# A list scheduler's choice on TensorE: 16-bit products ahead of float32 ones

## The chip, the cores and the metric

The kernel runs on one core of a Trainium2 chip. The metric is device time in microseconds (us); lower is better. Times are medians over runs, and one execution was also taken by the hardware profiler.

## The reference, cut to what matters

One step of an encoder trunk with one layer (`DEPTH = 1`) over 2048 prompt frames and 64 frames of a running stream, width 1024:

```python
h = rmsnorm(x, norm1_w)
proj = h @ w_in
# ... q, k, v (causal convolution, SiLU), z, decay a, beta b, pooling input u_pool
o, s_new = gated_delta_chunked(q, k, v, g, beta, s_prev, chunk)      # 4 heads of 128
o_delta = rmsnorm(o, onorm_w) * silu(z)
o_pool, pool_new = multiscale_pool(u_pool, pool_prev, pos0, pool_w, pool_scale)
x = x + concatenate([o_delta, o_pool]) @ w_out
h = rmsnorm(x, norm2_w)
x = x + (silu(h @ w_gate) * (h @ w_up)) @ w_down                     # d_ff = 2816
return rmsnorm(x, normf_w), ...                                      # and the new states
```

In `gated_delta_chunked` each chunk of a head needs the inverse `T` of a unit lower triangular matrix `eye + Lm`, and the state `S` is carried from chunk to chunk in order:

```python
T = triangular_solve(eye + Lm, eye)
...
v_new = u_c - w_c @ S
o_c = qd_c @ S + qk_c @ v_new
S = S * dl_c + kt_c.T @ v_new
```

## The kernel before, in words

The kernel first notes its instructions and only then issues them. Every call such as `nc.tensor.matmul(...)` goes to `Machine.note`, which records the operation with its predecessors, a cost and a rank. At the end `Machine.issue` walks through a planned time: at each step it takes the engine that can go first, takes one of that engine's ready operations, and sets down when it starts. The order in which operations are taken is the order in which each engine runs them on the chip. All of them are issued from one line, L278, so the profile's rows are told apart by their tiles.

The rank is the number under which an operation was noted, less a boost. Fronts and heads (below) are noted with a boost of 100000, so they have negative ranks and go ahead of the projections. A tile of a pool is given to an operation only when the planned time has freed one of that tag's buffers.

TensorE runs three kinds of products, set in `Machine.cost`: `"r"`, float32r operands; `"h"`, 16-bit operands; `"f"`, float32 operands and transposes. `Machine.pick` chooses among TensorE's ready ones. Products that are not `"r"` go ahead, but only in groups: while the last product was `"r"` and another `"r"` is ready, they are held until `HOLD` us after one of them became ready (0.4 for boosted ones, 3.0 for others). Once one has gone, the others that are ready follow it, by rank, until none is left.

The work has two parts.

- *First part, to about 945 us.* Four blocks of tokens (576, then three of 512). For each block: the input projection (`pp`, float32r, each operand split into a high and a low part, three products for one), four heads, four pooling groups, and the out-projection (`pz`) of the block before it, between the block's own projections. The last two blocks' out-projections come at the end; the third block's operands go through DRAM (`od`) and are loaded and split again (`op<-od`).
- *Second part.* Gate, up and down products in float32r (`px`, `py`, `pz`, `d`, `dx`, `dy`, `dz`), in a form with seven products in place of eight.

A head has two `Front`s, each for two chunks of 128 frames, and one serial chain. A front makes transposes (`ptk`, `ptv`, float32), Gram products (`gr`, float32), row sums (`gb`), and then doubles the inverse in seven levels (`py`, `pt`), with a correction (`pf`, `px` with the suffix `_p`); these levels are 16-bit. Between two of its products stands an operation of DVE or ACT that takes the result out of PSUM. The serial chain (`Head.prompt`) makes, for each chunk, the products `pk` (three) and `po` (two) in float32 with an ACT or DVE step between them, and ends with sums over squares (`os`, float32r) and a norm. A front's results wait in buffers (`NOUT = 5` and `NX = 3` of them) until the serial chain has used them.

Of the kernel before, what the change touches and what calls it, by code (L numbers as in the profile page):

```python
# [58 lines left out]
class Machine:  # L59
# [6 lines left out]
    def __init__(self, nc):  # L66
        self.nc, self.ops, self.seen, self.boost, self.n = nc, [], {}, 0, 0
        self.tiles, self.slots, self.queue, self.parked, self.later, self.early = {}, {}, {}, {}, {}, 0
        self.free = {e: 0.0 for e in ("tensor", "vector", "scalar", "gpsimd", "sync")}
        self.last, self.at = None, 0.0  # L70
        self.busy = {"vector": 0.0, "gpsimd": 0.0}
        self.wire = 0.0
        self.gone = 0.0
        for e in self.free:
            setattr(self, e, Engine(self, e))
# [205 lines left out]
    def pick(self, ready, t):  # L281

        others = sorted(x for x in ready if x[2].kind != "r")
        if others:
            first = others[0]
            held = self.last == "r" and len(others) < len(ready) and t < min(x[2].ready + HOLD[x[0] >= 0] for x in others)
            if held:
                first = min(x for x in ready if x[2].kind == "r")
            ready.remove(first)
            heapq.heapify(ready)  # L290
            return first[2]
        return heapq.heappop(ready)[2]

    def run(self, op, t):
        op.start = t
        if op.eng == "tensor":

            free, kind = self.free["tensor"], op.kind
            if self.last == kind and op.ready <= free:
                op.start = max(t, self.at + op.ldw)  # L300
            elif kind == "r":
                if op.ready <= free:
                    op.start = max(op.ready, free - (0.028 if self.last == "h" else 0.081))
                op.occ, op.lat = op.occ + 0.087, op.lat + 0.087
            elif self.last == "h":
                op.occ, op.lat = op.occ + 0.054, op.lat + 0.054
            else:
                op.occ, op.lat = op.occ + 0.02, op.lat + 0.02
            self.at, self.last = op.start, kind
            self.free["tensor"] = op.start + op.occ  # L310
        elif op.eng == "sync":
            self.free["sync"] = t + op.occ
            self.wire = max(self.wire, t + op.occ) + op.size / (
                (STORE if op.store else 400e3) if op.size > 300000 else 320e3)
            op.lat = self.wire + 1.35 - t
        else:
            if op.port:

                other = "gpsimd" if op.eng == "vector" else "vector"
                more = min(max(self.busy[other] - t, 0.0), op.occ)  # L320
                op.occ, op.lat = op.occ + more, op.lat + more
                self.busy[op.eng] = t + op.occ
            self.free[op.eng] = t + op.occ
# [32 lines left out]
def hybrid_kernel(ctx, tc, a, o):  # L356
# [61 lines left out]
    def drain(until=lambda: False):  # L418
        while chains and not until():
            c = min((c for c in chains if c.runnable()), key=lambda c: c.at)  # L420
            if c.at > clock["pe"]:
                clock["lost"] = clock.get("lost", 0) + c.at - clock["pe"]
                clock["pe"] = c.at
            c.step()
# [93 lines left out]
    ready, due, stored = [], [], set()  # L518
# [264 lines left out]
    def project(B, *ms):  # L783

        ws = [weights("win", m) for m in ms]

        out = [[bank(("ok", (1, 2))[m][i], f"pp{m}_{i}") if B.j == 0 and m < 2 else psmm(f"pp{B.j}_{m}_{lo}")
                for i, (lo, n) in enumerate(B.subs)] for m in ms]
        for ks in (range(4), range(4, KT)) if len(ms) > 1 else (range(KT),):
            for m, w, pss in zip(ms, ws, out):  # L790
                for (lo, n), ps in zip(B.subs, pss):
                    for k in ks:
                        one_k(B, m, w[k // 4], ps[:, :n], k, slice(lo, lo + n))
                        pump()
        return out if len(ms) > 1 else out[0]
# [469 lines left out]
    def fold_pool():  # L1265

        for g in range(4):
            ts(poolw[:, g, :], poolw[:, g, :], psc[:, g : g + 1], None, ALU.mult)
            for i in range(2):
                t = wpool.tile([P, 512], F32, tag="xs", name=f"fw{g}_{i}", bufs=XBUFS["xs"])  # L1270
                sl = slice(4 * i, 4 * i + 4)
                t3 = t.rearrange("p (m c) -> p m c", c=P)
                nc.sync.dma_start(out=t3, in_=a["wout"][sl, :, (4 + g) * P : (5 + g) * P].rearrange("m p c -> p m c"))
                yield 4.0
                ps = psg(f"fp{g}_{i}")
                mm(ps, poolw[:, g, :], t, start=True, stop=True)
                nc.scalar.copy(t, ps)
                nc.sync.dma_start(out=wpd[sl, :, g * P : (g + 1) * P].rearrange("m p c -> p m c"), in_=t3)
                yield LAT_APPLY

    def new_o(B, pool=None, tag="op", bufs=2):
        four = [(pool or opool).tile([P, 4, 2, MB], F32R, tag=tag or f"h{k}", name=f"op{k}_{B.j}", bufs=bufs) for k in range(2)]
        B.o, B.o4 = [four[k // 4][:, k % 4] for k in range(KT)], four[0]

    def pools(B):
        for gs in ((0,), (1,), (2,), (3,)) if B.dec else ((0,), (1,), (2, 3)):
            pps = project(B, *(17 + g for g in gs))
            for g, pp in zip(gs, pps if len(gs) > 1 else (pps,)):
                B.pools.append(Chain(pool_group(B, g, pp)))

    def out_proj(B):
        acts = [(k, B.o[k]) for k in (4, 5, 6, 7, 0, 1, 2, 3)]

        late = [0] if B.kept else []
        src = stream_x(a["xT"], "xc", B.t0, "xc")
        for ms in ((0, 1), *((m,) for m in range(2, KT))) if B.kept else ((m,) for m in range(KT)):
            ws = [weights("wout", m, *late) for m in ms]
            for lo, n in B.subs:
                xs = [src(m, lo, n) for m in ms]
                pss = [psmm(f"pz{B.j}_{m}_{lo}") for m in ms]  # L1300
                for part in (acts[:4], acts[4:]) if len(ms) > 1 else (acts,):
                    for w, ps in zip(ws, pss):
                        dense(ps, w, part, lo, n, first=part[0] is acts[0], last=part[-1] is acts[-1])
                for m, x, ps in zip(ms, xs, pss):
                    add_x(B, m, x, ps[:, :n], lo)
# [66 lines left out]
    for j in range(NBLK):  # L1372
        first = None
        if j:
            pab, first = project(B, 0, 1)
        else:
            pab = project(B, 0)
        machine.boost = HOT_ROWS
        rows(B, pab)
        machine.boost = 0  # L1380
        blocks.append(B)
        nxt = Block(j + 1) if j + 1 < NBLK else None
        B.heads, B.pools = [], []
        if prev is None or nxt is None:
            new_o(B)
        for h in range(NH):
            B.heads += head_project(B, h, first if h == 0 else None)
            heads.append(B.heads[h])
            if h == 1 and nxt is None:
                pools(B)  # L1390
            if h == OUT_AFTER and prev is not None and nxt is not None:
                drain(lambda: all(g.done for g in prev.heads) and all(c.done for c in prev.pools))
                out_proj(prev)
                if not B.kept:
                    new_o(B)
            if h == 1 and j == 0:
                fold = Chain(fold_pool())
            if h == 1 and nxt is not None:
                norm_stats(nxt)
            if h == STATS0 and nxt is None:  # L1400
                stats0 = Chain(stats2(0, gp, "ext", 4))
        if j == 0:
            fold.wait()
        if nxt is not None:
            pools(B)
            norm_apply(nxt)
        prev, B = B, (nxt if nxt is not None else B)
# [23 lines left out]
    for k in (4, 5, 6, 7, 0, 1, 2, 3):  # L1431
        t = wpool.tile([P, 512], F32, tag="xc", name=f"od{k}", bufs=XBUFS["xc"])
# [23 lines left out]
    for nm in FH[3:]:  # L1456
        t = f2.tile([P, 4, 2, N2], F32R, tag=f"h{nm}", name=f"hB{nm}")
# [168 lines left out]
    for op in order:  # L1626
        b = op[1]
        if op[0] == "gu":
            f = op[2]
# [38 lines left out]
WSCALE, FSCALE = 2048.0, 256.0  # L1668
BOOST = 100000

HOLD = 0.4, 3.0
BACKLOG, IDLE, AHEAD_OPS = 4.0, 0.0, 400

MARGIN = {"tensor": 0.25, "vector": 0.1, "scalar": 0.1, "gpsimd": 0.1, "sync": 3.0}
# [137 lines left out]
```

## Time and profile before

| what | us |
|---|---|
| median of 3 runs (2339.19 to 2341.5) | 2339.23 |
| the profiled execution | 2338.61 |
| its span, first to last instruction | 2336.8 |
| TensorE (PE) busy in it | 2301.8 |
| VectorE (DVE) busy | 1689.0 |
| ScalarE (ACT) busy | 1356.4 |
| GpSimd (POOL) busy | 843.6 |

The span has 41455 instructions. Busy time of PE is a union: products overlap in the array, so the start of the next product, not the duration of one, tells how long it holds the engine. PEld are the weight loads that run beside it. DMA is given as the mean busy share of 16 engines. An arrow `out<-in` names the tiles that an instruction writes and reads, and what stands after `<-` at a wait is what ended it.

### The profile page before, as it was taken

How to read it: one execution, taken by the hardware profiler on the slowest of the kernel's cores; microseconds unless marked ns; L12 is line 12 of the kernel's file. 1: busy time of each engine (PE TensorE's matmuls, PEld its weight loads, DVE VectorE, ACT ScalarE, POOL GpSimd, SP SyncE). 2: the span in 40 equal slices, each digit the busy share in tenths (PEclk: the TensorE clock that was granted, in tenths of full speed). 3: DMA queues.
4: the chain of work that ended last, by engine and by line, in shares of the span. 5: the costliest groups of instructions: out<-in, count | busy, mean ns of one | idle time of the engine just before them, and what ended most of it. 6: DMA issues, size and time to landing. Idle time of an engine off the chain costs nothing.

```text
span 2336.8 us, 41455 instructions
## 1 busy us (share of the span) xinstructions
PE 2301.8 (99%) x14614; PEld 2138.4 (92%) x14614; DVE 1689.0 (72%) x3097; ACT 1356.4 (58%) x3020; POOL 843.6 (36%) x963
## 2 busy tenths in 40 slices
PE   8999999999999999999999999999999999999998
PEld 7898898778777878999999999999999999999998
DVE  8998755664676786788667665877877868766776
ACT  6987856683767675655445465554444664454444
POOL 3434222430234530554322244643432653331312
PEclk9999999999999999999999999999999999999999
DMA  8755566545464577877545377768545586455453
GB/s 293 250 160 181 169 229 209 182 156 192 165 212 159 185 206 239 294 274 252 205 169 187 139 247 231 240 205 285 181 142 183 175 289 220 146 182 189 145 193 105
DMA packets 218881, 471.36 MB, mean 202 GB/s; under 512 B 27184, under 2 KB 85552, under 8 KB 218672
## 3 DMA queue, kind: packets, MB, share of 16 engines
q1 hardware_dynamic: 218672, 468.71, 60.9%
q8 instruction: 115, 1.88, 0.3%
q14 instruction: 94, 0.77, 0.1%
HBM read 354.81 MB, written 113.80 MB: 201 GB/s over the span
## 4 chain that ended last, share of the span: by engine, by line
PE 82%; DVE 9%; ACT 4%; DMA 3%; issue 2%; POOL 0%; SPq 0%; POOLq 0%; DVEq 0%; ACTq 0%
PE px L278 19%; PE pp L278 16%; PE pz L278 12%; PE py L278 8%; PE d L278 8%; PE dx L278 6%; PE dy L278 3%; PE pk_p L278 2%; PE pt_p L278 2%; DVE hq L278 2%; PE dz L278 1%; DVE y L278 1%; PE gr_p L278 1%; PE py_p L278 1%; ACT hr L278 1%
## 5 line engine op out<-in xcount | busy, mean ns | idle before, releaser
L278 PE MATMUL pp<-h,wsp 128*128 128x512 f32 (+1 forms) x2480 | 561.0, 366 | 11.6 <-DVE wsp L278 10.3
L278 PEld LDWEIGHTS pp<-h,wsp 128*128 128x128 f32 x2480 | 400.5, 189 | 59.1 <-ACT wsp L278 8.9
L278 ACT CAST ws<-wr 128x512 fp32r<-128x512 f32 x198 | 122.0, 618 | 172.9 <-PE dx L278 49.6
L278 DVE TENSOR_TENSOR ws<-wr,ws 128x512 fp32r<-128x512 f32 x198 | 164.2, 831 | 57.3 <-ACT ws L278 51.8
L278 PE MATMUL d<-h,wsd 128*128 128x352 f32 x1056 | 170.5, 322 | 0.0
L278 PE MATMUL pz<-op,wsp 128*128 128x288 f32 (+1 forms) x768 | 169.9, 357 | 0.3 <-DVE op L278 0.2
L278 PEld LDWEIGHTS d<-h,wsd 128*128 128x128 f32 x1056 | 168.7, 188 | 0.4 <-DVE h L278 0.4
L278 ACT ACTIVATE hr<-g 128x352 f32<-128x352 f32 x132 | 65.7, 497 | 163.8 <-DVE g L278 163.5
L278 ACT CAST TV_p<-pt_p 128x512 f16<-128x512 f32 x192 | 111.1, 589 | 62.2 <-PE pt_p L278 61.7
L278 PE MATMUL px<-hA,ws 128*128 128x352 f32 x792 | 144.7, 322 | 0.7 <-DVE ws L278 0.7
L278 PE MATMUL py<-hB,wsS 128*128 128x352 f32 x792 | 143.8, 322 | 0.0
L278 PE MATMUL px<-hBT,wsS 128*128 128x352 f32 x792 | 139.6, 324 | 3.0 <-ACT g L278 2.6
L278 PE MATMUL pz<-hB,ws 128*128 128x352 f32 x792 | 142.5, 322 | 0.0
L278 PE MATMUL py<-hA,wsS 128*128 128x352 f32 x792 | 139.8, 322 | 0.0
L278 PE MATMUL px<-hBT,ws 128*128 128x352 f32 x792 | 138.1, 322 | 1.3 <-DVE u L278 1.3
L278 POOL TENSOR_TENSOR wrS<-wr,wrS 128x512 f32<-128x512 f32 x44 | 63.0, 1431 | 207.7 <-DMA wr<-in_wg_dram 64.2
L278 PE MATMUL px<-hA,wsS 128*128 128x352 f32 x792 | 137.8, 322 | 0.0
L278 PEld LDWEIGHTS px<-hBT,wsS 128*128 128x128 f32 x792 | 128.2, 188 | 7.4 <-ACT g L278 7.3
L278 PEld LDWEIGHTS px<-hA,ws 128*128 128x128 f32 x792 | 129.8, 188 | 1.2 <-DVE ws L278 1.0
L278 PEld LDWEIGHTS px<-hBT,ws 128*128 128x128 f32 x792 | 128.6, 188 | 2.3 <-DVE u L278 2.2
L278 PEld LDWEIGHTS py<-hB,wsS 128*128 128x128 f32 x792 | 129.8, 188 | 0.0
L278 PEld LDWEIGHTS pz<-hB,ws 128*128 128x128 f32 x792 | 129.6, 188 | 0.0
(686 smaller groups left out, 5606.3 us busy)
## 6 DMA issues: line engine op xcount, KB each, us to landing
wsS<-gS SPq DMA_DIRECT2D x176, 512.0 KB, 4.6
wsp<-wnd SPq DMA_DIRECT2D x126, 512.0 KB, 3.4
gS<-wsS SPq DMA_DIRECT2D x88, 512.0 KB, 4.4
wr<-in_wg_dram SPq DMA_DIRECT2D x132, 256.0 KB, 3.1
wnd<-wsp SPq DMA_DIRECT2D x42, 512.0 KB, 5.0
xd<-x2d SPq DMA_DIRECT2D x96, 176.0 KB, 3.8
wr<-in_wu_dram SPq DMA_DIRECT2D x66, 256.0 KB, 3.6
wrd<-in_wd_dram SPq DMA_DIRECT2D x56, 256.0 KB, 3.6
```

What stands on the lines that cost most here:

```text
L278: getattr(getattr(self.nc, op.eng), name)(*args, **kw)
```

## The change

Among the waiting products that are not `"r"`, `pick` takes the first one by rank whose kind is not `"f"`, and one of kind `"f"` only when no 16-bit one is ready. Whether they are held is asked through a new function `hold`, which gives a third value of `HOLD` to boosted operations that were noted before a mark; the mark, `calm`, is set when the last block's first head has been noted. The third value is 0.4.

```diff
-        self.last, self.at = None, 0.0
+        self.last, self.at, self.calm = None, 0.0, 0
...
         others = sorted(x for x in ready if x[2].kind != "r")
         if others:
-            first = others[0]
-            held = self.last == "r" and len(others) < len(ready) and t < min(x[2].ready + HOLD[x[0] >= 0] for x in others)
+            first = min(others, key=lambda x: (x[2].kind == "f", x))
+            held = self.last == "r" and len(others) < len(ready) and t < min(x[2].ready + self.hold(x) for x in others)
             if held:
                 first = min(x for x in ready if x[2].kind == "r")
...
+    def hold(self, x):
+
+        return HOLD[2] if x[0] < 0 and x[2].order < self.calm else HOLD[x[0] >= 0]
...
+            if (j, h) == (3, 0):
+                machine.calm = len(machine.ops)
...
-HOLD = 0.4, 3.0
+HOLD = 0.4, 3.0, 0.4
```

All other lines are the same, and so are the operations that are noted; their order differs, on TensorE and, since the planned times move, on the other engines and the DMA queue too.

## The prediction

> **What bounds the kernel now.** I read the profile in this order: the page's busy shares and its chain, then the table by stage, then the order of TensorE's products in one stage, then what stands around the last head.
>
> ```profile
> PE 2301.8 (99%) x14614; PEld 2138.4 (92%) x14614; DVE 1689.0 (72%) x3097; ACT 1356.4 (58%) x3020; POOL 843.6 (36%) x963
> ...
> PE 82%; DVE 9%; ACT 4%; DMA 3%; issue 2%; POOL 0%; SPq 0%; POOLq 0%; DVEq 0%; ACTq 0%
> ```
>
> TensorE is busy for 2301.8 of 2336.8 us, and 82% of the chain that ended last is TensorE itself. So the time is, first of all, the sum of what the products take in the order in which they stand. Reordering them can change two things only: what it costs to go from one kind of product to another, and how long TensorE has nothing ready.
>
> The table by stage (columns: the stretch in us, its length, then busy us and instructions of PE, PEld, DVE, ACT, POOL, granted clock, DMA share, GB/s) shows where it has nothing ready:
>
> ```profile
> 91.00:214.00 123.00, 122.75 (x1064) 113.61 (x1063) 112.64 (x269) 105.21 (x274) 51.77 (x84) 1.00 0.54 173
> 214.00:242.00 28.00, 26.54 (x144) 20.89 (x143) 24.91 (x50) 16.74 (x38) 7.21 (x12) 1.00 0.81 253
> 242.00:352.00 110.00, 109.49 (x821) 97.82 (x820) 72.07 (x152) 73.54 (x178) 28.46 (x40) 1.00 0.59 200
> 352.00:665.00 313.00, 312.61 (x1882) 248.85 (x1881) 180.80 (x376) 194.86 (x467) 89.49 (x139) 1.00 0.55 180
> 665.00:700.00 35.00, 33.97 (x201) 26.82 (x199) 29.79 (x52) 24.00 (x52) 13.20 (x18) 1.00 0.69 229
> 700.00:832.00 132.00, 131.94 (x808) 103.32 (x807) 92.57 (x185) 98.83 (x247) 64.81 (x87) 1.00 0.56 171
> 832.00:850.00 18.00, 16.60 (x116) 11.50 (x116) 15.04 (x33) 15.28 (x39) 8.53 (x8) 1.00 0.66 191
> 850.00:902.00 52.00, 52.00 (x322) 43.44 (x321) 34.26 (x68) 26.06 (x56) 8.90 (x10) 1.00 0.64 203
> ```
>
> Length less busy PE is idle: 0.25, 1.46, 0.51, 0.39, 1.03, 0.06, 1.40 and 0.00 us, together 5.10 us from 91 to 902 us. The granted clock is 1.00 throughout, so no wait here is made dearer by a slower clock. I chose these stretches because the listing of TensorE's order (14185 products in both kernels) first differs at the product that ran at 91 us in the profile of before, and 16-bit and float32 products of the first part end at 902 us. After that the listing only exchanges whole groups of 12 float32r products up to about 1180 us; from there all orders are equal. What happens before 91 and after 1180 us is thus the same work in the same order.
>
> **The change, part by part.** *The hold.* `HOLD` gets a third value and `hold` chooses it for early boosted work, but the third value is 0.4, the same as the first. So `calm` changes nothing, and I cost it at exactly zero.
>
> *Sixteen-bit before float32.* In `pick`, the first of the waiting products is no longer the one of lowest rank, but the first 16-bit one, and a float32 one only where no 16-bit one is ready. I call a run of 16-bit and float32 products between two float32r ones a visit. Counted in the listings, before to after: visits 447 to 437; visits that begin with 16-bit 273 to 320; that end with 16-bit 302 to 222; that end with float32 145 to 215; places inside a visit where float32 follows 16-bit 111 to 182; where 16-bit follows float32 140 to 84. No product is added or removed. What each such place costs is read from starts in the timeline of TensorE (first column start, last the count of records; f16 is 16-bit; pk, po and ptv are float32, and one pk or po is two records; pp is float32r, though written f32):
>
> ```profile
> 670.78 0.34 PE L278 MATMUL px_p<-TV_p,TV1F_p 128*128 128x128 f16 x3
> 670.96 0.28 PE L278 MATMUL pt_p<-Yt_p,TV_p 128*128 128x128 f16 x2
> 671.07 0.28 PE L278 MATMUL pt_p<-TV_p,Yt_p 128*128 128x128 f16 x2
> 671.18 0.44 PE L278 MATMUL pk_p<-Sp,Yqk 128*128 128x128 f32 x2
> 671.46 0.39 PE L278 MATMUL po_p__2069<-Qd_p,Sp 128*128 128x128 f32 x2
> 671.60 0.95 PE L278 MATMUL pp<-h,wsp 128*128 128x512 f32 x3
> 672.39 0.28 PE L278 MATMUL px_p<-YtF_p,TV1F_p 128*128 128x128 f16 x2
> 672.51 0.44 PE L278 MATMUL pk_p<-rhs_p,X_p 128*128 128x128 f32 x2
> 672.79 0.28 PE L278 MATMUL py_p<-TV_p,Wh_p 128*128 128x128 f16 x2
> 672.87 1.18 PE L278 MATMUL pp<-h,wsp 128*128 128x512 f32 x4
> 673.88 0.38 PE L278 MATMUL ptv_p<-consts,Yvz 128*128 128x128 f32 x2
> 674.10 0.39 PE L278 MATMUL pk_p<-vn_p,ktl_p 128*128 128x128 f32 x2
> 674.33 0.39 PE L278 MATMUL po_p__2069<-Gam_p,vn_p 128*128 128x128 f32 x2
> 674.55 0.28 PE L278 MATMUL pt_p<-Yt_p,TV_p 128*128 128x128 f16 x2
> 674.66 0.28 PE L278 MATMUL pt_p<-TV_p,Yt_p 128*128 128x128 f16 x2
> 674.74 3.00 PE L278 MATMUL pp<-h,wsp 128*128 128x512 f32 x12
> 677.59 0.28 PE L278 MATMUL py_p<-TV_p,Wh_p 128*128 128x128 f16 x2
> ```
>
> - One more visit. Twelve pp from 674.74 to the next row take 2.85 us, four from 672.87 take 1.01. Eight products make the difference of 1.84, so one takes 0.23 and the first after a visit 0.32: 0.09 us a visit. Ten fewer: -0.9 us.
> - Leaving by a 16-bit product. The pair of pt at 674.55 takes 0.11, the pair at 674.66 before pp 0.08: the float32r product starts 0.03 us early. Eighty fewer: +2.4 us.
> - Leaving by a float32 product. po at 674.33 takes 0.22, po at 671.46 before pp 0.14: 0.08 us saved. Seventy more: -5.6 us.
> - Float32 after 16-bit. pk at 671.18 and at 672.51 take 0.28, pk at 674.10 after another float32 takes 0.23: 0.05 us. Seventy-one more: +3.6 us.
> - 16-bit after float32. po at 674.33 takes its full 0.22 and the pt behind it their 0.11: nothing, so the 56 fewer bring nothing.
> - Entering by 16-bit. The three px at 670.78 take 0.06 each, a pt pair 0.11, so 0.01 us. Forty-seven more: +0.5 us.
>
> The sum is 0.0 us. Each price is read to 0.01 us; were all of them off by that to one side, it would be 2.8 us (80 + 70 + 71 + 47 + 10 places), so the bounds are -2.8 and +2.8. I take 0.0, because the prices come from the same 7 us and repeat in it.
>
> That is the first surprise of this working: grouping by kind looks as if it saved changes of kind, but the visits stay as many. What is gained by leaving through a float32 product is paid back where float32 stands behind 16-bit.
>
> [...]
>
> ```profile
> L278 PEld LDWEIGHTS <-Wh_p 128*128 128x128 f16 x512 | 38.4, 98 | 27.7 <-issue 20.6 <-ACT TV_p L278 0.6 <-ACT ext L278 0.5
> L278 PEld LDWEIGHTS pk_p<-Sp,Yqk 128*128 128x128 f32 x128 | 21.6, 189 | 2.5 <-DVE Sp L278 0.2
> ```
>
> [...] A load of 0.189 us can't hide behind one 16-bit product of 0.055 (half a pt pair). If all that sticks out counted, float32 behind 16-bit would cost 0.134 us and not 0.05; this is a rival below. The timeline's pk shows 0.05.
>
> *What waits behind.* A float32 product that is ready now lets a batch of py (2) or pt (4) go ahead, 0.11 to 0.22 us by the rows above. On the float32 side stand the transposes (`ptk`), the Gram products (`gr`) and the serial state chain of each head (`pk`, `po`). Behind pk wait ACT's vn and DVE's rhs and S, and behind the end of the state chain wait the buffers of later fronts (`NOUT`, `NX`). In the listing this is to be seen: head (1,0) ends (its product os) 59 float32r products later than before, (3,0) 22, (3,1) 27, (3,2) 17, (3,3) 11. But both listings have issued the same 861 16-bit and float32 products when the 1571st float32r one comes (352 us), and the same number again at 572, 665 and 905 us. Until then TensorE works on float32r products in their place, so the lag costs nothing there; the cover is the stock of ready float32r products. Without cover a lag of 59 products is worth
>
> ```profile
> L278 PE MATMUL pz<-op,wsp 128*128 128x288 f32 x384 | 60.6, 302 | 0.0
> ```
>
> 60.6 / 384 = 0.158 us each, 9.3 us. That is the upper bound of this term; the lower one is below nothing, all 5.10 us of idle gone.
>
> *Stages with little cover.* In 832 to 850 us the out-projection waits for the splits of `od`, and 16-bit work fills. After the change there are 73 16-bit and 6 float32 products before pz's 22nd product, where there were 77 and 15: nine float32 products at 0.25 us (between 0.22 and 0.28), 2.25 us less filling. Against this stands ACT's order:
>
> ```profile
> 832.18 0.63 ACT L278 ACTIVATE Gam_p<-gb_p,EC 128x128 f32<-128x128 f32 x2
> ...
> 834.35 0.64 ACT L278 COPY Yvz<-pp 128x512 f32<-128x512 f32 x1
> ...
> 835.01 0.67 ACT L278 CAST op<-od 128x512 fp32r<-128x512 f32 x1
> ```
>
> Before, ACT did Gam_p and the squares of the last head's ptk (32 to 35 us past 800) ahead of the first op<-od at 835.01. In the new listing that split stands ahead of them, and could start near 832.2: 2.8 us earlier. The two cancel within 0.6 us, and I take nothing. On SP the stores and loads of the second part's statistics (hpd, xd) move ahead of some od loads; DMA is 0.66 busy in that stage, and from the fourth on these loads wait for a buffer that a split frees, so nothing is charged.
>
> *The last head.* Its output is split here, while TensorE is in the last out-projection:
>
> ```profile
> 902.54 43.72 PE L278 MATMUL pz<-op,wsl 128*128 128x512 f32 x192
> ```
> ```profile
> L278 DVE TENSOR_TENSOR op<-osq_p__2855,op x1: 681/681/681, 908.0 to 908.0; 128x512 fp32r<-128x512 f32 x1
> ```
>
> The first 72 of these 192 products don't need it. At 43.72 / 192 = 0.228 us each they end at 918.9; the split ends at 908.7. That is 10.2 us of slack, and 11 products later take 2.5 of it. Nothing is late.
>
> **The sum.** 0.0 from the order and 0.0 from waits. The profiled execution took 2338.61 us (span 2336.8 and 1.8 around it), 0.6 below the median of the runs. Carried to the median: 2339.2 us. A measurement of this kernel can tell some 0.2%, 4.7 us, from no change.
>
> **Rivals.**
> - *Idle goes.* With the 16-bit chains of a front going first, fronts are ready where the splits starve TensorE (214, 665, 832 us). For it: these chains are what fills there. Against it: the same products have to wait for the same splits, and DVE is busy 24.91 of 28.00 us in the first of them. All 5.10 us gone gives 2334.1.
> - *Slower: the state chain comes late.* Float32 products that free buffers are put off, and a starved stage finds no fronts to work on. The place is 832 to 850 us; it decides if the splits end last there in spite of their earlier start. Price between 2.25 us and the 9.3 of an uncovered lag; I take 6, about the middle, as both are equally far from a row that shows it: 2345.2. For it: the lags of 11 to 59 products. Against it: the counts are equal again at 352 and 905 us.
> - *Slower: loads stick out.* At 0.134 us in place of 0.05 for 71 more places, 9.5 and not 3.6: +5.9, 2345.1. Against it: the 0.28 of pk.
>
> That the order stays as it was can be excluded: 3470 of 14185 places differ.
>
> **Chances and range.** Forecast 0.66, with smaller forms of the others in it; idle gone 0.15; late state chain 0.16; loads 0.03. So faster by over 0.2% 0.15, within 0.66, slower 0.19. The range goes from 2334.5 to 2345.5: the idle rival lies just below, and half of the late chain's prices above, so under 2 in 10 is left out.
>
> **What would show it.** In the profile of after: PE's busy time within 2.8 us of 2301.8; idle in 91 to 902 us near 5 us; starts as above (pk 0.28 behind a 16-bit product, po 0.14 before pp); the first op<-od within a microsecond of the last pp; the rows after 1180 us alike but for a shift. I am wrong if PE's idle in the three starved stages grows by over 4 us, or if busy time moves by over 3.

## The result, and the profile after

| | before | after |
|---|---|---|
| median us (15 runs each) | 2339.84 (2338.51 to 2344.61) | 2346.03 (2342.88 to 2348.74) |
| ratio to before, 95% interval | | 1.0025 (1.0017 to 1.0033) |
| the profiled execution | 2338.61 | 2345.86 |
| its span | 2336.8 | 2344.1 |

The change costs 6.2 us, 0.26%. I had forecast 2339.2 with a range up to 2345.5, and had given slower a chance of 0.19. The time lies 6.8 us above the forecast and 0.5 us above the range.

The page of after, its busy shares and its chain:

```profile
PE 2304.1 (98%) x14614; PEld 2132.9 (91%) x14614; DVE 1688.2 (72%) x3097; ACT 1354.7 (58%) x3020; POOL 856.9 (37%) x963
...
PE 78%; DVE 10%; ACT 4%; issue 3%; DMA 3%; POOL 1%; SPq 0%; DVEq 0%; POOLq 0%; ACTq 0%
```

TensorE is busy 2.3 us longer and idle 5.0 us longer (span less busy: 35.0 before, 40.0 after); these two executions are 7.3 us apart, 1.1 more than the medians. The table by stage tells where the idle time came in (columns as before: stretch, length, PE busy, then PEld, DVE, ACT and POOL, granted clock, DMA share, GB/s):

```profile
91.00:214.00 123.00, 122.86 (x1060) 112.43 (x1059) 111.19 (x266) 104.85 (x273) 53.82 (x84) 1.00 0.55 175
214.00:242.00 28.00, 25.57 (x143) 20.16 (x142) 26.18 (x50) 16.85 (x39) 8.74 (x11) 1.00 0.82 253
...
352.00:665.00 313.00, 313.00 (x1888) 247.66 (x1887) 183.37 (x377) 195.31 (x469) 92.49 (x139) 1.00 0.56 181
665.00:700.00 35.00, 34.90 (x209) 27.47 (x209) 30.32 (x54) 24.49 (x51) 15.69 (x17) 1.00 0.72 228
700.00:832.00 132.00, 129.36 (x783) 100.25 (x782) 95.72 (x174) 93.72 (x234) 67.94 (x88) 1.00 0.55 170
832.00:850.00 18.00, 14.32 (x86) 9.88 (x85) 15.25 (x31) 15.92 (x45) 6.85 (x8) 0.91 0.63 192
850.00:902.00 52.00, 52.00 (x341) 40.91 (x340) 34.32 (x74) 27.09 (x61) 9.56 (x10) 1.00 0.60 184
...
985.00:1030.00 45.00, 41.98 (x256) 40.53 (x255) 40.69 (x51) 30.73 (x68) 29.52 (x22) 1.00 0.85 296
```

Idle of PE from 91 to 902 us went from 5.1 to 9.1 us. Stage by stage: 214 to 242 us 1.46 to 2.43; 665 to 700 us 1.03 to 0.10; 700 to 832 us 0.06 to 2.64; 832 to 850 us 1.40 to 3.68, and there the granted clock is 0.91 where it was 1.00. In 985 to 1030 us, where the two orders differ by whole groups of float32r products only, idle is 3.02 us. It was 1.25 before:

```profile
985.00:1030.00 45.00, 43.75 (x268) 42.53 (x267) 42.50 (x57) 33.84 (x74) 25.78 (x19) 1.00 0.89 312
```

A second reading follows one product: the start of the n-th float32r product in after, less its start in before. It compares equal work only where both have issued the same number of other products: +0.1 us at 352 us, -1.0 at 665, +4.2 at 902, +5.7 at 1008 and +6.2 at 1185 us. (In between other products are put off, nine at 760 us and 28 at 849 us, so a value there is neither a loss nor a gain yet.) So the reordered stretch up to 665 us costs nothing. The next one, to 902 us, costs 5.2 us. By the two tables 3.9 us of it are idle time of TensorE (6.4 less 2.5 us); the rest is what one stretch at half clock costs, 1.3 us as worked out below. Some 2 us more come where the second part begins. From 1185 us on, where both orders are equal, these two executions part by another 1.1 us without more idle time, which the medians don't show.

The waits of TensorE from 665 to 905 us in after (us in total, times, longest):

```profile
PE gb_p L278 <- ACT ktl_p L278: 1.6, 1, 1.6
PE px_p L278 <- ACT TV1F_p L278: 1.4, 1, 1.4
...
PE py_p L278 <- ACT TV_p L278: 0.6, 2, 0.4
PE gb_p L278 <- ACT TV_p L278: 0.5, 1, 0.5
PE py_p L278 <- ACT ktl_p L278: 0.5, 1, 0.5
PE gr_p L278 <- ACT Gam_p L278: 0.4, 1, 0.4
```

Five of these six lines lie in 832 to 850 us, and none of them is a wait for a split of `od`. The timelines show what TensorE had at hand. First before, PE (start, length of the group, product, count):

```profile
826.50 0.39 PE L278 MATMUL ptk_p<-consts,Yqk 128*128 128x128 f32 x2
...
828.98 0.34 PE L278 MATMUL gb_p<-Ghl,selp 128*128 128x256 f32 x1
...
830.71 0.27 PE L278 MATMUL gb_p<-negm,idbf 128*128 128x256 bf16 x1
830.74 1.40 PE L278 MATMUL pp<-h,wsp 128*128 128x512 f32 x5
...
832.33 0.44 PE L278 MATMUL ptk_p<-consts,Yqk 128*128 128x128 f32 x2
832.86 1.13 PE L278 MATMUL gr_p<-Yqk 128*128 128x256 f32 x4
...
835.74 0.49 PE L278 MATMUL pz<-op,wsp 128*128 128x512 f32 x1
```

Then after, PE, and ACT in the same microseconds:

```profile
828.51 1.86 PE L278 MATMUL pp<-h,wsp 128*128 128x512 f32 x7
...
831.21 0.47 PE L278 MATMUL pz<-op,wsp 128*128 128x512 f32 x1
...
836.98 1.17 PE L278 MATMUL pz<-op,wsp 128*128 128x512 f32 x4
837.99 0.52 PE L278 MATMUL ptk_p<-consts,Yqk 128*128 128x128 f32 x3
...
840.46 0.38 PE L278 MATMUL gb_p<-Ghl,selp 128*128 128x256 f32 x1 [1.62 <-ACT ktl_p L278]
841.36 0.27 PE L278 MATMUL gb_p<-negm,idbf 128*128 128x256 bf16 x1 [0.52 <-ACT TV_p L278]
842.13 0.27 PE L278 MATMUL py_p<-TV_p,Wh_p 128*128 128x128 f16 x2 [0.51 <-ACT ktl_p L278]
```
```profile
837.33 0.63 ACT L278 ACTIVATE E<-Yvz 128x512 f32<-128x512 f32 x1 [1.04 <-DVE Yqk L278]
838.00 0.72 ACT L278 ACTIVATE E<-E,onec 128x512 f32<-128x512 f32 x1
838.75 0.63 ACT L278 ACTIVATE E<-E 128x512 f32<-128x512 f32 x1
839.28 0.26 ACT L278 ACTIVATE ktl_p<-ptk_p 128x128 f32<-128x128 f32 x1
```

By the order in which the kernel issues them, the transposes (`ptk`) at 826.50 are those of the last head's first front; its row sums (`gb`) follow at 828.98 and 830.71, its Gram products (`gr`) at 832.86. (The transposes at 832.33 belong to the second front.) So before, that front's first steps lie among the last products of the input projection (`pp`), and TensorE has work while ACT makes what each step needs. After, the last `pp` are those at 828.51, the out-projection starts at 831.21 and is fed early, and the front's transposes come at 837.99, 11.5 us later. The square sums that wait for them (`ktl`) stand on ACT behind a group of three SiLU steps (`E`), which itself waited 1.04 us for DVE. From 838.8 us on the next product in TensorE's queue waits four times, for ACT each time: the three shown, and `gr_p` for `Gam_p`.

### The profile page after: what moved, and what is told of

The parts are those of the page before. It is cut to its first block, busy times and chain, and to the rows that moved or that the text cites. A ratio compares the mean times of both kernels' runs of the same rounds, so it can differ in the third digit from the quotient of the medians.

```text
span 2344.1 us, 41452 instructions
## 1 busy us (share of the span) xinstructions
PE 2304.1 (98%) x14614; PEld 2132.9 (91%) x14614; DVE 1688.2 (72%) x3097; ACT 1354.7 (58%) x3020; POOL 856.9 (37%) x963
## 4 chain that ended last, share of the span: by engine, by line
PE 78%; DVE 10%; ACT 4%; issue 3%; DMA 3%; POOL 1%; SPq 0%; DVEq 0%; POOLq 0%; ACTq 0%
PE px L278 17%; PE pp L278 16%; PE pz L278 11%; PE d L278 8%; PE py L278 7%; PE dx L278 5%; PE dy L278 3%; PE pk_p L278 2%; PE pt_p L278 2%; DVE y L278 2%; DVE hq L278 2%; PE dz L278 1%; PE gr_p L278 1%; ACT hr L278 1%; DMA hpd<-xt 1%
## 5 line engine op out<-in xcount | busy, mean ns | idle before, releaser
L278 PE MATMUL pp<-h,wsp 128*128 128x512 f32 (+1 forms) x2480 | 557.7, 366 | 10.8 <-DVE wsp L278 9.2
L278 PEld LDWEIGHTS px<-hA,wsS 128*128 128x128 f32 x792 | 128.8, 188 | 1.2 <-ACT g L278 1.2
```

Source lines behind the costliest of these rows:

```text
L278: getattr(getattr(self.nc, op.eng), name)(*args, **kw)
```

## The experiments

All ratios are to the kernel before, run beside; its median there was 2340.55 us (e1 to e3, n_42), 2340.36 (s1 to s4), 2341.19 (s5, n_45, r_36, r_45), 2340.66 (n_36, n_38, r_38, r_42) and 2339.84 (r_front_late, s7). "Idle" is length less busy of PE in the profiled execution; the clock is the granted one in 832 to 850 us. The kernels `n_` lack the rule, the kernels `r_` have it; the `s` kernels are spliced from both orders. A profile is of one execution; those of e1, r_36 and r_front_late are 1.3, 1.6 and 2.5 us below their medians.

| kernel | median us | ratio, 95% interval | idle 91 to 902 | idle 832 to 850 | clock there |
|---|---|---|---|---|---|
| before | 2339.84 | | 5.1 | 1.40 | 1.00 |
| after | 2346.03 | 1.0025 (1.0017 to 1.0033) | 9.1 | 3.68 | 0.91 |
| s1, after to 665 us | 2339.03 | 0.9995 (0.9986 to 1.0003) | 4.9 | 1.27 | 0.91 |
| s7, after to 693 us | 2339.06 | 0.9996 (0.9987 to 1.0006) | 5.1 | 1.26 | 1.00 |
| s5, after to 800 us | 2343.34 | 1.0011 (1.0002 to 1.0020) | 7.5 | 1.37 | 1.00 |
| s3, after to 905 us | 2345.43 | 1.0020 (1.0012 to 1.0029) | 8.7 | 3.68 | 0.91 |
| s2, after from 665 us | 2346.41 | 1.0026 (1.0015 to 1.0037) | 7.6 | 3.86 | 0.81 |
| s4, after from 905 us | 2341.46 | 1.0005 (0.9996 to 1.0014) | 5.1 | 1.84 | 1.00 |
| e1, rule in blocks 0 to 2 | 2345.19 | 1.0020 (1.0011 to 1.0028) | 9.3 | 3.33 | 1.00 |
| e2, rule in the last block | 2345.92 | 1.0026 (1.0016 to 1.0035) | 8.5 | 3.97 | 0.91 |
| e3, other order on ACT | 2347.42 | 1.0031 (1.0020 to 1.0043) | 9.9 | 4.81 | 1.00 |
| r_front_late | 2345.22 | 1.0018 (1.0009 to 1.0027) | 7.3 | 1.02 | 1.00 |
| n_36 | 2346.43 | 1.0024 (1.0015 to 1.0034) | 7.1 | 3.06 | 0.91 |
| r_36 | 2348.27 | 1.0030 (1.0019 to 1.0040) | 9.0 | 3.11 | 0.91 |
| n_38 | 2352.66 | 1.0047 (1.0034 to 1.0061) | 10.3 | 3.23 | 0.73 |
| r_38 | 2351.18 | 1.0046 (1.0033 to 1.0058) | 10.2 | 3.18 | 0.73 |
| n_42 | 2347.42 | 1.0027 (1.0015 to 1.0038) | 7.0 | 3.54 | 0.91 |
| r_42 | 2349.75 | 1.0038 (1.0026 to 1.0051) | 10.5 | 3.87 | 0.93 |
| n_45 | 2348.20 | 1.0035 (1.0021 to 1.0049) | 11.7 | 4.57 | 1.00 |
| r_45 | 2349.30 | 1.0037 (1.0024 to 1.0050) | 10.8 | 3.15 | 1.00 |

**The rule in one part of the program.** e1 applies it while every waiting product was noted before the mark `calm`, e2 from there on:

```diff
-            first = min(others, key=lambda x: (x[2].kind == "f", x))
+            first = min(others, key=lambda x: (x[2].kind == "f" and all(y[2].order < self.calm for y in others), x))      # e1
+            first = min(others, key=lambda x: (x[2].kind == "f" and any(y[2].order >= self.calm for y in others), x))     # e2
```

e1: 

> 16-bit first only while all waiting products were noted before the last block's second head; from then on by rank as before (orders equal those of after up to the product at 683 us). Theory A (the loss sits in a few waits of the last block and behind it, at 781, 838 to 844 and 1003 us of after's profile): 2338 to 2341 us, within 2 us of before. Theory B (the rule costs along its whole length, because float32 work is put off): 50 of the 71 added float32-behind-16-bit places are kept, so some +4 us, 2344. Theory C (any re-planned order moves the time by a few us either way, whatever the rule): anywhere from 2336 to 2346.

e2: 

> The other half alone: by rank as before up to the last block's first head, 16-bit first from then on. Theory A: nearly the whole loss, 2343 to 2347 us. Theory B: 30 of the 71 places, about +2, 2342. Theory C: anywhere from 2336 to 2346.

Either half loses nearly the whole amount, 4.6 and 5.4 us. The losses don't add up as those of two parts of one price would (theory B, 2344 and 2342), and e1 is not within 2 us of before either (theory A). In both, the stage from 832 to 850 us is idle as in after, also in e1, where the rule isn't at work in the last block any more but the plan had moved before it.

**One order on ACT.** e3 keeps after's order on TensorE and moves the three SiLU steps of the last head, and the DVE product behind them, behind the square sums:

```diff
+        late = [op for op in out if writes(op, "scalar", "E2_3_3_")] + [...]   # ...: the DVE product that reads them
+        out = [op for op in out if op not in late]
+        at = max(i for i, op in enumerate(out) if writes(op, "scalar", "kn_p3_3_0", "kn_p3_3_1"))
+        out[at + 1 : at + 1] = late
```

> After's order on TensorE unchanged; on ACT the three steps of one silu (E2 of the last head) are moved behind the squares of the last head's ptk, with the DVE product that uses them. So ptk's bank is read about 2 us earlier and gb, which blocked TensorE from 838.8 to 840.5 us, waits less. Theory A: the wait shrinks by 1.5 to 2 us and the stretch of 3.4 us at half clock goes (worth up to 1.7 us): 2342 to 2343.5. Theory B: the time stays within 1 us of after's 2346. If only the wait is worth something and the clock nothing: 2344 to 2344.5.

No gain: 2347.42 us, above all that was expected. The half-clock stretch is gone (clock 1.00 in the stage), and idle rose all the same to 4.81 us: TensorE now waits 1.8 us for `TV_p` of ACT and 0.8 us for `ktl_p`. So making the longest wait shorter brought nothing; the time went into other waits for ACT in the same stage.

**Another plan without the rule.** n_42 is the kernel before with `HOLD = 0.42, 3.0`:

> A re-plan without the rule: before with its first HOLD at 0.42 in place of 0.4. Visits stay 447, and 3639 of 14185 places of TensorE's order differ. Theory A and B: within 2 us of before. Theory C: moves by 3 us or more, either way.

It loses 6.9 us without the rule, as only theory C allowed, and idle in 832 to 850 us is 3.54.

**Where in the order.** Five kernels are the kernel before with the issue order written out: up to a float32r product of a given number it is that of one kernel on every engine, behind it that of the other.

```diff
+        by = {op.order: op for op in out}
+        out = [by[i] for i in ORDER]        # ORDER: the list of numbers, which the kernel unpacks from a literal
```

s1: 

> A splice of the two issue orders: all operations that before issues ahead of its 2620th float32r product (665 us; both kernels have then issued the same products) stand in after's order, the rest in before's order. It keeps 2220 of the reordered stretch's float32r products, and roughly two thirds of the added float32-behind-16-bit places. Place theory (the loss arises after 665 us): within 1.5 us of before, rather faster (after's trace is 1.0 us ahead there): 2338 to 2340.5. Rule theory (putting float32 off costs everywhere): +4, about 2344.

s2: 

> The complement: before's order up to 665 us, after's from there on. Place theory: the whole loss of after and the 1.0 us that it had gained: +6 to +8, 2346 to 2348. Rule theory: a third of it, +2, 2342.

s3: 

> After's order up to 905 us (the 3344th float32r product, end of the 16-bit and float32 work), before's order behind it. Place theory with two places (832 to 850 us, and the start of the second part at 1003 us): the second place is undone, +4 of after's +6: 2343.5 to 2345. If the second place only follows from the first part's state: as after, 2346.

s4: 

> Before's order up to 905 us, after's behind it, where no product changes kind and only groups of 12 and the other engines' orders differ. Place theory with two places: +2 us, 2341.5 to 2343. If the second place only follows from the first part's state: as before, within 1 us.

s5: 

> The order on every engine is the changed kernel's up to the 3027th float32r product (about 800 us) and the earlier kernel's from there on. Theory A (the loss is made inside 800 to 905 us, by what is left to fill the stage in which the out-projection waits for the splits of od): within 2 us of the kernel before, 2338 to 2341 us, and TensorE's idle in 830 to 857 us near 1.4 us. Theory B (the loss is made earlier, by products that the rule puts off before 800 us and that are made up later): about 2345 us, as with the changed order to 905 us (2345.4).

The stage of s1 and the whole of the first part in it (windows of s1, columns as above):

```profile
832.00:850.00 18.00, 16.73 (x108) 11.62 (x107) 14.94 (x32) 14.28 (x36) 7.63 (x8) 0.91 0.68 187
91.00:902.00 811.00, 806.15 (x5347) 664.16 (x5346) 561.32 (x1180) 554.13 (x1348) 281.24 (x395) 1.00 0.59 187
```

After's order to 665 us costs nothing (s1, the interval reaches from -3.3 to +0.7 us), although 48 of the 71 added places where float32 follows 16-bit lie there. After's order from 665 us on costs the whole (s2), after's to 905 us some 5 (s3), after's from 905 us some 1 us, which its interval doesn't tell from none (s4). In s2 and s3 the stretch from 665 to 902 us adds up as in after: 5.3 us longer than before in s2, with 2.5 us more idle and two stretches at half clock, and 4.3 in s3, with 2.8 us more idle and one. The stage's idle falls into two groups: 1.26 to 1.84 us in the five kernels with before's order there (s7, told of below, among them), 3.33 and up in those with after's or e1's or e2's. s5 expected 2338 to 2341 by the theory that the stage alone decides, and 2345 by the other; it came out between. Its stage is as before, but a new wait came at the seam:

```profile
760.00:830.00 70.00, 66.87 (x380) 52.87 (x378) 50.22 (x89) 45.53 (x102) 34.92 (x42) 0.95 0.53 165
```
```profile
802.83 0.80 PE L282 MATMUL os_p__2642<-hi_p__2643,ones 128*128 128x512 f32 x1 [2.45 <-ACT hi_p__2643 L282]
```

Here a head's state chain is late by after's order, and before's order behind the seam puts its last product where it isn't ready: one wait of 2.45 us, and the mean clock from 760 to 830 us falls to 0.95. s5 therefore doesn't settle which part of 665 to 905 us carries what.

**More filling, less filling, with and without the rule.** Between the 3134th and the 3171st float32r product (that stage) before has 78 products of the other kinds, after 55. I took that number for the cause and tested it by plans that leave more or fewer, made by the value of `HOLD` alone:

```diff
-HOLD = 0.4, 3.0, 0.4
+HOLD = 0.36, 3.0, 0.36        # r_36; r_38, r_42, r_45 alike
-HOLD = 0.4, 3.0
+HOLD = 0.45, 3.0              # n_45; n_36, n_38, n_42 alike, without the rule
```

r_36: 

> The changed kernel with HOLD 0.36, 3.0, 0.36 in place of 0.4, 3.0, 0.4: the rule is kept, and its new plan leaves 82 products of 16-bit and float32 between the 3134th and the 3171st float32r product (78 in the kernel before, 55 in the changed one). Theory A (what decides is the filling left for the starved stage): within 2 us of the kernel before, 2338 to 2342 us, stage 832 to 850 us losing no more than before. Theory C (the rule itself costs, wherever it reorders): about 2346 us.

r_45: 

> The changed kernel with HOLD 0.45, 3.0, 0.45: the rule is kept, and 49 filling products are left in that stage (55 in the changed one). Theory A: 2346 us or more, the stage losing 3 us or more against the kernel before. Theory C: about 2346 us too. If it is within 2 us of the kernel before, the count of filling products doesn't tell the stage's loss.

n_45: 

> The kernel before, without the rule, with HOLD 0.45, 3.0: 53 filling products are left in that stage (78 with 0.4). Theory A: slow although the rule is absent, 2344 to 2348 us, the loss in 832 to 850 us. Theory C: within 2 us of the kernel before, 2338 to 2342 us.

The theory of filling fell with r_36: 82 products are there, and the stage is idle for 3.11 us with a clock of 0.91. The theory that the rule costs wherever it reorders had n_45, which has no rule, within 2 us of before; it takes 2348.2 us, so a loss of this size needs no rule. The stage in n_45:

```profile
832.00:850.00 18.00, 13.43 (x93) 9.54 (x92) 15.13 (x32) 15.35 (x44) 4.16 (x6) 1.00 0.72 169
```

The order of issue of these kernels tells more than the count. In the six with 1.84 us or less of idle from 832 to 850 us, the transposes of the last head's first front start some 5 us ahead of the last `pp`; in the fourteen with 3.06 us or more they start behind it, by 0.3 to 11 us. First r_front_late (told of below; 1.02 us idle), then r_36 (3.11 us), where the four `ptk` of both fronts follow the last `pp`:

```profile
831.11 0.38 PE L278 MATMUL ptk_p<-consts,Yqk 128*128 128x128 f32 x2
...
835.80 0.71 PE L278 MATMUL pp<-h,wsp 128*128 128x512 f32 x2
```
```profile
834.48 0.95 PE L278 MATMUL pp<-h,wsp 128*128 128x512 f32 x3
835.27 0.68 PE L278 MATMUL ptk_p<-consts,Yqk 128*128 128x128 f32 x4
```

So what goes with the stage's idle is whether that front begins under the input projection, and not how many products are left. Five of the six have before's order there and four of the fourteen after's, and no run moves these transposes alone: this is read from the traces and not tested.

**The pairs completed.** So a rival was left: any new plan of this kernel loses, and the rule has no price of its own.

n_36: 

> The kernel before, without the rule, with HOLD 0.36, 3.0. Partner of the run with the rule at 0.36, which took 2348.3 us. The kernel's own planned time ends at 2336.9 us here. Theory D (any new plan loses to waits that the plan doesn't hold, and the rule has no price of its own): 10.9 to 13.6 us above the planned end, as the seven new plans run so far, so 2347.8 to 2350.5 us. Theory C (the rule costs some 6 us wherever it is): about 2342 us.

n_38: 

> The kernel before, without the rule, with HOLD 0.38, 3.0; planned end 2335.7 us. Theory D: 2346.6 to 2349.3 us, and within 2 us of its partner with the rule. Theory C: 2340 to 2343 us, some 6 us below its partner.

r_38: 

> The changed kernel with HOLD 0.38, 3.0, 0.38; planned end 2334.6 us. Theory D: 2345.5 to 2348.2 us. Theory C: 2346 to 2348 us as well; the difference to the partner without the rule tells.

r_42: 

> The changed kernel with HOLD 0.42, 3.0, 0.42; planned end 2334.0 us. Its partner without the rule took 2347.4 us. Theory D: 2344.9 to 2347.6 us, at or below the partner. Theory C: about 2353 us.

With the rule less without it, by medians: +1.8 us at 0.36, -1.5 at 0.38, +2.3 at 0.42, +1.1 at 0.45; the ratios differ by 0.0006, -0.0001, 0.0011 and 0.0002, and the intervals of each pair overlap. Only at 0.40 is it +6.2. A price of 6 us wherever the rule stands is excluded; the mean of the four is about +1 us, which these runs don't tell from none. My band for the new plans (10.9 to 13.6 us above the end of the kernel's own planned time) was too narrow: the four came out at 9.5 (n_36), 17.0 (n_38), 16.6 (r_38) and 15.8 us (r_42). What held is that the kernel before stands alone: 5.6 us above its planned end (2334.2), and every other plan 9.5 to 17. Their loss isn't waiting alone. In n_36 TensorE is busy 6.5 us longer than before, of a span 7.8 us longer:

```profile
0.00:2400.00 2400.00, 2308.35 (x14614) 2140.34 (x14614) 1685.40 (x3097) 1355.60 (x3020) 845.18 (x963) 1.00 0.60 196
```

It has 466 visits (447 before), 1.7 us at the prediction's price of 0.09 us, and two stretches at half clock.

**The state chain alone, and a version to beat both.** r_front_late lets only the fronts' float32 products stand back, and leaves `pk` and `po` their rank (in the cut below `name(x)` stands for the name of the tile that the product writes); s7 is s1 with the seam at the 2704th float32r product.

```diff
-            first = min(others, key=lambda x: (x[2].kind == "f", x))
+            first = min(others, key=lambda x: (x[2].kind == "f" and not name(x).startswith(("pk", "po")), x))
```

r_front_late: 

> The changed kernel, but only the float32 products of the fronts (ptk, ptv, gr) stand back behind 16-bit ones; those of the state chain (pk, po) keep their rank. Planned end 2332.0 us, the earliest of all. Theory D (a new plan ends 10.9 to 13.6 us above its planned end): 2342.9 to 2345.6 us. Theory E (my rival of the prediction: it is the late state chain that costs): within 2 us of the kernel before, 2338 to 2342 us.

s7: 

> The changed kernel's order on every engine up to the 2704th float32r product (about 693 us), the earlier kernel's from there on: a try at a version that beats both. The trace of the changed kernel is 2.4 us ahead at that place, that of the run with the changed order to 665 us was 1.2 us ahead. If nothing is lost behind it, 2337 to 2338.5 us against some 2340 for the kernel before; if the half-clock stretch in 832 to 850 us comes back as in that run, 2338 to 2339.5.

r_front_late has the earliest planned end of all (2332.0 us) and took 2345.2, 13.2 above it, as theory D had it. It doesn't take the late state chains away: by its order of issue head (1,0) still ends 41 float32r products later than before, and head (3,1) 27, as in after. So it can't say what the loss would be without them. But its stage from 832 to 850 us is idle for 1.02 us only, less than before, so a head (3,1) as late as in after doesn't starve that stage by itself:

```profile
832.00:850.00 18.00, 16.98 (x117) 11.58 (x115) 17.19 (x37) 17.47 (x49) 6.93 (x8) 1.00 0.71 193
```

It loses elsewhere: its idle from 91 to 902 us is 7.3 us. s7 has the clock at 1.00 in the stage and takes 2339.06 us, s1 2339.03, against 2339.84 and 2340.36 of before beside them; neither is told from no change, and s7 misses the 2337 to 2338.5 us hoped for, so there is no version here that measurably beats the kernel before.

## Why the prediction was wrong, by its own steps

- *The hold costs zero.* No run speaks against it; it changes no order.
- *The order, 0.0 within 2.8 us.* Right as far as it can be read. TensorE's busy time rose by 2.3 us, within the bound, and part of that is the half clock below. At 665 us, with the same products issued in both, after is 1.0 us ahead. The prices hold in after:

```profile
670.03 0.28 PE L278 MATMUL pt_p<-TV_p,Yt_p 128*128 128x128 f16 x2
670.14 0.44 PE L278 MATMUL pk_p<-Sp,Yqk 128*128 128x128 f32 x2
670.42 0.39 PE L278 MATMUL po_p__2069<-Qd_p,Sp 128*128 128x128 f32 x2
670.56 0.95 PE L278 MATMUL pp<-h,wsp 128*128 128x512 f32 x3
```

  pk behind a 16-bit pair takes 0.28 us, po ahead of pp 0.14, as forecast. With that the rival of the loads that stick out (+5.9 us) falls; s1 says the same with 48 of its 71 places.
- *"The lag costs nothing there."* Right to 665 us (s1), where a head ends 59 products later. Not right for the last block: there the lag that shows is not of the state chain but of the transposes of the last head's first front, 11.5 us, and no stock of ready products covers it.
- *"The two cancel within 0.6 us, and I take nothing."* This is the step that failed. Both of its halves came true: fewer products to fill, and the out-projection started 4.5 us earlier (831.21 for 835.74; I had 2.8 for its split). But they don't cancel: the term that I put at nothing measured 3.6 us, 2.28 of idle and 1.3 for a stretch at half the clock. An earlier split lets TensorE use up its `pz` early, and then the front whose transposes have been put off behind the last `pp` waits for ACT step by step. Being put off behind the out-projection's start is not needed for it: in e2, n_36, n_38, n_42, n_45, r_36 and r_38 these transposes come ahead of the first `pz`, but behind the last `pp`, and the stage is idle for 3.06 to 4.57 us. I counted products and asked whether the splits come last; I did not ask what stands at the head of TensorE's queue in each microsecond and what ACT does ahead of it.
- *"So no wait here is made dearer by a slower clock."* True of before, and I carried it over to after. In after:

```profile
837.00:840.40 3.40, 1.84 (x15) 1.32 (x12) 2.42 (x5) 3.00 (x10) 0.83 (x1) 1.00 1.06 394
840.40:843.80 3.40, 1.89 (x11) 1.29 (x12) 2.02 (x5) 3.40 (x19) 1.66 (x3) 1.00 0.85 291
843.80:847.20 3.40, 3.40 (x12) 2.24 (x12) 3.00 (x11) 2.45 (x6) 0.67 (x1) 0.50 0.42 131
847.20:850.60 3.40, 3.40 (x29) 2.50 (x27) 3.40 (x7) 3.37 (x8) 3.27 (x3) 1.00 0.41 98
```

  Behind 6.8 us in which PE is busy for 3.7, the clock is granted at 0.50 for one stretch of 3.4 us. Its price is read from s1, which runs before's order in the stage with such a stretch and no more idle time: it is 1.24 us ahead of before at 832 us and 0.05 behind at 849, so the stretch costs 1.29 us.
- *On SP "nothing is charged".* In after's profile a transfer is at the root of the 1.42 us that TensorE waits at 783 us. POOL, then ACT:

```profile
779.55 0.94 POOL L278 TENSOR_TENSOR xt<-xd,xd 128x352 f32<-128x352 f32 x1 [6.72 <-DMA hpd<-xt]
780.45 1.73 POOL L278 TENSOR_TENSOR osq_p__2489<-osq_p__2489,Yvz 128x512 f32<-128x512 f32 x1
```
```profile
782.21 0.62 ACT L278 CAST op<-osq_p__2489 128x512 fp32r<-128x512 f32 x1 [2.39 <-POOL osq_p__2489 L278]
782.74 0.41 ACT L278 ACTIVATE TV1F_p<-TV32F_p 128x256 f16<-128x256 f32 x1
```

  A store (`hpd`) holds up POOL, behind it stands a head's output, behind that on ACT the split, and behind the split the operand that TensorE wants next. From 700 to 832 us, where I charged nothing, after is idle for 2.6 us more than before. This is not a constant of the order: s2 and s3, with the same order there, are idle for 0.25 us from 760 to 830 us, after for 1.69.
- *The rows after 1180 us, and the start of the second part.* I took the work before 91 us and after 1180 us for equal, and the exchange of whole groups in between for free. At 1005.21 us TensorE waits 1.81 us for DVE's `u` (0.72 before, at 1000.30). s4, which has only this part of the change, doesn't tell its price from none, and s1 loses 1.3 us at the same place with before's own order. So a part of this is scatter between executions.
- *Buffers.* I had the late state chain free `NOUT` and `NX` late. With a larger `NX` or `NOUT` the listings of both kernels, on every engine, stay as they are: these buffers order nothing in the plan. No run has more of them.
- *The rivals.* The slower rival, "the state chain comes late", had the place (832 to 850 us), a stage with no front ready and a price near the measured one (2345.2 us, against 2346.0), but hardly the mechanism: in r_front_late head (3,1) ends as late as in after and the stage isn't starved, and the waits of after's stage are at a front's first steps. Its chance of 0.16 was too low, and that a place and a price so near came out of it is luck. My test, idle in the three starved stages up by over 4 us or busy by over 3, would not have shown the loss either: the three grew by 2.3 us together and busy by 2.3. Most of the rest came in a stretch that had had no idle, 700 to 832 us, and at the start of the second part.

What is shown: most of the loss, 5.2 us, sits from 665 to 902 us and is idle time and one stretch at half clock; it isn't the price of the changes of kind; a price of the rule in every plan is excluded; and of ten plans, at five values of `HOLD` with and without the rule, one alone takes 2340 us, and the change leaves just that one. What is not shown is what makes that plan the good one. For the starved stage the traces point to the place of the last head's first front, but r_front_late has that and loses elsewhere; neither the filling nor ACT's order around the longest wait explains it. The missing case in the prediction was: *the order that is left behind has few waits of its own, and a new one can have more.* I gave "same" 0.66 because I took every step near nothing; the nine other plans lie 5.8 to 12.0 us above the kernel before.

## What to carry to other kernels

When a scheduler fixes the order, a small rule is a new plan everywhere behind its first difference. Cost the new plan, not the rule: walk through the stages in which an engine was nearly starved, and ask for each what stands at the head of every queue, not only how many products are left to fill. Before crediting or blaming a rule, run it and its absence at neighbouring values of a parameter that also makes a new plan: here one pair gave +6.2 us, and four others -1.5 to +2.3.

## What the runs showed of the hardware that was not expected

In after TensorE's clock is granted at 0.50 from 843.8 to 847.2 us, behind short waits that only thin its work out: the two rows of 3.4 us ahead of this stretch are busy for 1.84 and 1.89 us, as the profile counts busy, each product with its whole duration. The longest single wait there was 1.62 us. How busy TensorE was doesn't tell alone: the row with 1.84 us is followed by one at full clock, the row with 1.89 us by the one at half, and in n_45 a stretch at half clock follows one that is busy for 2.38 us:

```profile
687.70:691.10 3.40, 2.38 (x17) 1.94 (x17) 3.31 (x10) 0.97 (x3) 1.54 (x2) 1.00 0.50 154
691.10:694.50 3.40, 3.40 (x15) 2.85 (x15) 2.44 (x4) 1.97 (x4) 1.99 (x4) 0.50 0.00 0
```

Such a stretch also came with before's own order: s1, which has that order from 665 us on, has one in 832 to 850 us (mean clock 0.91), where before has none (1.00). In n_38 and r_38 the mean clock in 832 to 850 us is 0.73, and these are the slowest kernels of all (2352.66 and 2351.18 us).
